# Way up of both MLPs as pairs of column groups in seven block products

## The chip, the cores and the metric

The program runs on one NeuronCore of a Trainium2 chip, in one launch. The metric is the device time of that core in microseconds (us). In the rows PE is TensorE (matmuls; PEld its weight loads), DVE is VectorE, ACT is ScalarE, POOL is GpSimd, and SP is the engine that issues most DMAs.

## The reference, cut to what matters

Two layers work on 640 tokens (128 of a context, 512 of a latent grid) of width 1024, with different weights per layer. A layer is three parallel mixers, an output projection, and a gated MLP:

```python
xn2 = rmsnorm(x, norm2) * (1 + scale2) + shift2
u = dwconv3(xn2 @ w_up, ffn_conv_w)          # w_up: 1024 x 5632, conv of width 3 over positions
a, bval = u[..., :D_FF], u[..., D_FF:]       # D_FF = 2816
x = x + gate2 * ((jax.nn.silu(a) * bval) @ w_down)
```

`shift2`, `scale2` and `gate2` come from a conditioning vector times `w_ada` (6144 columns per layer), one set for the context and one for the grid. All is float32.

## The kernel before

Activations lie with channels on the 128 partitions and the 640 tokens along the free axis: `x` is eight tiles [128, 640]. Each float32 operand of a product is split into two float32r parts, high and low, and a product is three matmuls: high weights by high input (L150), high by low (L151), low by high (L152). The tokens go in two halves of 320, the columns of one matmul. A piece of weights [128, 512] (four blocks of 128 rows of the contraction) comes by DMA into `wraw` (4 buffers); `split` (L114 to L116) makes `whi` on ScalarE and then `wlo = wraw - whi` on VectorE (6 buffers each).

The MLP (from L1017) goes in four parts of `FFPARTS`. In each part it computes the way up of 5 or 6 pairs of column groups, a gate group and its value group of 128 columns each, and then the way down from those tiles. Group by group, `up_half` puts eight blocks times three matmuls per half of the tokens into a PSUM tile `f`. `ffn_conv` (L806 to L810) takes it from PSUM: ScalarE scales it by the middle tap into `u`, and VectorE adds the other two taps, for the 128 and the 512 tokens apart. `ffn_act` makes silu on ScalarE, the product (L816) on VectorE, and the split `fh`, `fl` for the way down.

At the start of an MLP the output projection has just ended for the second half of the tokens. The first half of the normalised input is made during that projection (`norm_steps`, tiles `Xh`, `Xl`). For the second half, a few matmuls by ones add up the squares (L231), a chain of small VectorE instructions takes their inverse root (L213 to L219), a matmul spreads it (L243), and `norm_tile` writes the tiles one after the other. Meanwhile TensorE takes the first half of three groups (`lead`).

In the mixers of layer 0 and in its MLP, VectorE also computes modulations (`ada_rows`, L312): a step is one DMA of weights into `wraw` and two multiply-and-sum instructions, 84 steps in layer 0's mixers and 76 in its MLP.

The program is written with tile pools, and a scheduler sets each engine's order when it is built. At run time every engine takes its instructions in that order and waits on semaphores. So an instruction whose input is late holds up all that stands behind it on its engine.

## Time and profile before

| | |
|---|---|
| median of 3 runs | 2590.2 us (2588.8 to 2591.19) |
| profiled execution | span 2587.0 us from first to last instruction; the page gives no other time of it |
| TensorE, ScalarE, VectorE, GpSimd busy | 2536.4, 1067.8, 1698.1, 131.5 us |
| MLP of layer 0, of layer 1, first matmul of the way up to the end of the way down | about 456 us and 458 us |

What lies outside the span, median of the runs less span, is 3.2 us. A matmul's duration includes its way through the array and overlaps with that of its neighbours: durations of matmuls can't be added up, their starts tell the pace. On VectorE too, the next instruction can start before the last has ended; "slot" below means the time from one start to the next.

### The profile page before, as it was taken

What the parts mean: (1) busy time and instruction counts of PE and PEld (TensorE: products, weight loads), DVE (VectorE), ACT (ScalarE), POOL (GpSimd) and SP (SyncE); (2) the same over time, 40 slices, a digit from 0 to 9 for tenths busy, and PEclk for the clock granted to TensorE, in tenths of its full rate; (3) what the DMA queues carried; (4) which work ended last, traced back from release to release, by engine and by line L of the source; (5) the groups of instructions that cost most, each with busy time, mean ns of one, the idle gap of its engine ahead of it and who ended that gap; (6) DMA issues with size and microseconds to landing.
All of it is one profiled execution on the core that took longest, in us unless ns stands there. A gap on an engine that the chain in (4) does not pass through costs nothing. (4 is left out here: it accounts for less than half of the span.)

```text
span 2587.0 us, 44571 instructions
## 1 busy us (share of the span) xinstructions
PE 2536.4 (98%) x17422; PEld 2481.9 (96%) x17422; DVE 1698.1 (66%) x3627; ACT 1067.8 (41%) x2108; POOL 131.5 (5%) x113
## 2 busy tenths in 40 slices
PE   7999999999999999999999999999999999999998
PEld 3999999999999999999999999999999999999998
DVE  5677787787765878787667675555554466554555
ACT  3476733433324423232355666434333343233332
POOL 1000000000111000000010000000011110000001
PEclk8999999999999999999999999999999999999999
DMA  6211243333343334443331112212222312322221
GB/s 232 73 46 45 67 134 111 103 115 108 118 155 102 106 116 136 133 124 124 96 112 53 38 50 70 66 57 63 64 64 85 116 55 60 93 66 83 66 86 62
DMA packets 138597, 236.17 MB, mean 91 GB/s; under 512 B 16465, under 2 KB 34321, under 8 KB 138257
## 3 DMA queue, kind: packets, MB, share of 16 engines
q1 hardware_dynamic: 133778, 222.83, 27.9%
q10 hardware_dynamic: 4608, 10.49, 1.2%
q8 instruction: 137, 2.24, 0.3%
q14 instruction: 74, 0.61, 0.1%
HBM read 226.67 MB, written 6.59 MB: 90 GB/s over the span
## 5 line engine op out<-in xcount | busy, mean ns | idle before, releaser
L116 DVE TENSOR_TENSOR wlo<-wraw,whi 128x512 fp32r<-128x512 f32 (+1 forms) x620 | 407.9, 662 | 379.7 <-ACT whi L115 372.4
L115 ACT CAST whi<-wraw 128x512 fp32r<-128x512 f32 (+1 forms) x620 | 364.4, 592 | 659.8 <-PE f L151 345.7
L150 PE MATMUL lin<-Xh,whi 128*128 128x320 f32 x1920 | 605.3, 315 | 3.9 <-DVE th L573 2.6
L151 PE MATMUL lin<-Xl,whi 128*128 128x320 f32 x1920 | 595.7, 310 | 0.0
L152 PE MATMUL lin<-Xh,wlo 128*128 128x320 f32 x1920 | 595.6, 310 | 0.0
L150 PE MATMUL f<-Xh,whi 128*128 128x320 f32 x1408 | 435.4, 309 | 0.0
L151 PE MATMUL f<-Xl,whi 128*128 128x320 f32 x1408 | 435.2, 309 | 0.0
L152 PE MATMUL f<-Xh,wlo 128*128 128x320 f32 x1408 | 435.1, 309 | 0.0
L150 PEld LDWEIGHTS lin<-Xh,whi 128*128 128x128 f32 x1920 | 361.5, 188 | 5.4 <-DVE th L573 3.7
L151 PEld LDWEIGHTS lin<-Xl,whi 128*128 128x128 f32 x1920 | 361.8, 188 | 0.0
L152 PEld LDWEIGHTS lin<-Xh,wlo 128*128 128x128 f32 x1920 | 361.2, 188 | 0.0
L151 PEld LDWEIGHTS f<-Xl,whi 128*128 128x128 f32 x1408 | 264.3, 188 | 0.1
L150 PEld LDWEIGHTS f<-Xh,whi 128*128 128x128 f32 x1408 | 264.3, 188 | 0.0
L152 PEld LDWEIGHTS f<-Xh,wlo 128*128 128x128 f32 x1408 | 264.3, 188 | 0.0
L151 PE MATMUL f<-fl,whi 128*128 128x320 f32 x604 | 186.2, 309 | 0.0
L152 PE MATMUL f<-fh,wlo 128*128 128x320 f32 x604 | 185.2, 309 | 0.0
L150 PE MATMUL f<-fh,whi 128*128 128x320 f32 x604 | 182.2, 310 | 0.0
L312 DVE SCALAR_TENSOR_TENSOR ad<-wraw,rows 128x512 f32<-128x512 f32 x168 | 119.8, 713 | 47.5 <-DMA wraw<-in_w_rows 45.4
L312 DVE SCALAR_TENSOR_TENSOR pr<-wraw,rows 128x512 f32<-128x512 f32 x152 | 104.5, 688 | 26.0 <-DMA wraw<-in_w_rows 24.2
L150 PE MATMUL lin<-yh,whi 128*128 128x320 f32 x384 | 120.5, 314 | 0.7 <-ACT th L567 0.7
L152 PE MATMUL lin<-yh,wlo 128*128 128x320 f32 x384 | 118.8, 309 | 0.0
L151 PE MATMUL lin<-yl,whi 128*128 128x320 f32 x384 | 118.6, 309 | 0.0
(275 smaller groups left out, 4440.0 us busy)
## 6 DMA issues: line engine op xcount, KB each, us to landing
wraw<-in_w_main SPq DMA_DIRECT2D x456, 256.0 KB, 2.6
wraw<-in_w_rows SPq DMA_DIRECT2D x160, 256.0 KB, 2.7
wraw<-in_w_down SPq DMA_DIRECT2D x64, 256.0 KB, 2.7
wraw<-in_w_o SPq DMA_DIRECT2D x48, 256.0 KB, 2.6
ada<-in_w_ada SPq DMA_DIRECT2D x24, 256.0 KB, 6.0
x<-in_xT ACTq DMA_DIRECT2D x16, 320.0 KB, 3.3
wraw<-in_w_down SPq DMA_DIRECT2D x32, 128.0 KB, 2.1
wraw<-in_w_q SPq DMA_DIRECT2D x16, 192.0 KB, 2.3
```

Of the source, the lines that this page charges most:

```text
L115: S.copy(hi, x)
L116: V.tensor_tensor(lo, x, hi.bitcast(F32), ALU.subtract)
L150: PE.matmul(o, wh, xh[:, half(j)], start=(k == 0), stop=False)
L151: PE.matmul(o, wh, xl[:, half(j)], start=False, stop=False)
L152: PE.matmul(o, wl, xh[:, half(j)], start=False, stop=(k == n - 1))
L312: V.scalar_tensor_tensor(spare(), raw, 1.0, rows[:, s], ALU.mult, ALU.mult, accum_out=part[:, j, m - m0, s:s + 1])
```

## The change

A pair's two groups are computed together. The pair's weights are four blocks `wa`, `wb` (gate group, first and second half of the contraction) and `wc`, `wd` (value group); the normalised input is four blocks `B11`, `B21` (first half of the tokens; first and second half of the contraction) and `B12`, `B22`. Instead of eight block products, seven are made (a block product is 4 blocks of contraction times 3 matmuls): `wa`·`B11`, `wb`·`B21`, (`wa+wc`)·`T3`, (`wa+wc+wd`)·`t2`, `wd`·`T4`, (`wc+wd`)·`t1`, (`wa+wb+wc+wd`)·`B22`, where `T3`, `t2`, `T4`, `t1` are sums and differences of the blocks of input. Two PSUM banks, `Y` and `Z`, collect several of them, and what they hold in between is read out on the way.

- The sums of weights are four VectorE additions per pair, and seven pieces of weights are split instead of four. Pairs 0 to 2 of a layer (`LEAD`) load `wb` twice.
- Results are put together in SBUF (`o0`, `o1`, `z`): five ScalarE copies from PSUM and three VectorE instructions per pair. `ffn_conv` then reads SBUF and not PSUM.
- `Forms` makes the blocks of input: `first` during the output projection, `second` (with all sums and differences and ten splits of 640 columns) for the second half of the tokens, before any of the way up in program order.
- Of the modulations, 64 steps go from layer 0's MLP to layer 1's mixers; 12 stay.
- In the last part of a way down, five column tiles' weights are loaded and split again for the second half of the tokens instead of being kept.

```diff
@@
+DMA_ADDS = False
+LEAD = 3
...
-        BUFS = {"mla": {"sc": 2, "pt": 2}, "hgrn": {"sc": 2, "m": 1, "ad": 1}, "ffn": {"f": 3}}
+        BUFS = {"mla": {"sc": 2, "pt": 2}, "hgrn": {"sc": 2, "m": 1, "ad": 1}, "ffn": {"Y": 2, "Z": 2, "X": 2}}
...
+    KH = KD // 2
+    def form_tile(pool, dt, tag, name, bufs):
+        return pool.tile([P, 2, HALF], dt, tag=tag, name=name, bufs=bufs)
+    def norm_raw(l, which, sq, j, f, e, i, bc):
+        for s0, s1, s in SEGS[j]:
+            b0, b1 = s0 - j * HALF, s1 - j * HALF
+            V.scalar_tensor_tensor(f[:, e, b0:b1], x[i][:, s0:s1], amul[l][:, which, i, s:s + 1],
+                                   bc[:, b0:b1], ALU.mult, ALU.mult)
+            S.activation(f[:, e, b0:b1], f[:, e, b0:b1], AF.Identity, bias=modT[l][:, 24 * which + i, s:s + 1])
+    class Forms:
+        def __init__(self, l, which, sq, xf):
+            self.l, self.which, self.sq, self.xf = l, which, sq, xf
+            self.f = {n: [None, None] for n in ("B11", "B21", "B22", "t1", "t2", "T3", "T4")}
+            self.raw = {}
+        def put(self, name, q, f):
+            if name in ("t2", "T3", "T4"):
+                hi = form_tile(self.xf, R32, "Fh", "Fh", 6)
+                lo = form_tile(self.xf, R32, "Fl", "Fl", 6)
+            else:
+                hi = form_tile(mp, R32, "Xh", "Xh", 8)
+                lo = form_tile(mp, R32, "Xl", "Xl", 8)
+            split(f, hi, lo)
+            self.f[name][q] = (hi, lo)
+        def operand(self, name):
+            return [(self.f[name][r // 2][0][:, r % 2], self.f[name][r // 2][1][:, r % 2]) for r in range(KH)]
+        def first(self):
+            bc = self.sq.rstd(0)
+            for q in range(2):
+                for n, name in enumerate(("B11", "B21")):
+                    f = form_tile(mp, F32, "Xl", "xn", 8)
+                    for e in range(2):
+                        norm_raw(self.l, self.which, self.sq, 0, f, e, KH * n + 2 * q + e, bc)
+                        yield
+                    self.put(name, q, f)
+                    self.raw[name, q] = f
+        def second(self, pool):
+            bc = self.sq.rstd(1)
+            raw = self.raw
+            for q in range(2):
+                for n, name in enumerate(("B12", "B22")):
+                    f = raw[name, q] = form_tile(pool, F32, "fh", "xn", 7)
+                    for e in range(2):
+                        norm_raw(self.l, self.which, self.sq, 1, f, e, KH * n + 2 * q + e, bc)
+                f = raw["T3", q] = form_tile(pool, F32, "fl", "xs", 7)
+                V.tensor_tensor(f, raw["B22", q], raw["B12", q], ALU.subtract)
+                self.put("T3", q, f)
+            for q in range(2):
+                f = raw["t2", q] = form_tile(pool, F32, "fl", "xs", 7)
+                V.scalar_tensor_tensor(f, raw["T3", q], -1.0, raw["B11", q], ALU.mult, ALU.subtract)
+                self.put("t2", q, f)
+            for q in range(2):
+                f = raw["t2", q]
+                V.scalar_tensor_tensor(f, f, -1.0, raw["B21", q], ALU.mult, ALU.subtract)
+                self.put("T4", q, f)
+            for q in range(2):
+                f = raw["B12", q]
+                V.tensor_tensor(f, raw["B11", q], f, ALU.subtract)
+                self.put("t1", q, f)
+            for q in range(2):
+                self.put("B22", q, raw["B22", q])
+            raw.clear()
+    def part_product(o, W, X, start, stop):
+        wh, wl = W
+        for k, (xh, xl) in enumerate(X):
+            c = slice(k * P, (k + 1) * P)
+            PE.matmul(o, wh[:, c], xh, start=start and k == 0, stop=False, skip_group_check=True)
+            PE.matmul(o, wh[:, c], xl, start=False, stop=False, skip_group_check=True)
+            PE.matmul(o, wl[:, c], xh, start=False, stop=stop and k == KH - 1, skip_group_check=True)
+    def pair_steps(l, g, F, pool, lead, banks, evict):
+        wa, wb, wc, wd = (a["w_main"][l, gg, j] for gg in (g, g + 1) for j in range(2))
+        def load(src, own=False):
+            t = (pool.tile([P, 512], F32, tag="T", name="T", bufs=LEAD) if own else
+                 wp.tile([P, 512], F32, tag="wraw", name="wraw", bufs=RAWB))
+            nc.sync.dma_start(t, src)
+            return t
+        def form(t):
+            hi = wp.tile([P, 512], R32, tag="whi", name="whi", bufs=WB)
+            lo = wp.tile([P, 512], R32, tag="wlo", name="wlo", bufs=WB)
+            split(t, hi, lo)
+            return hi, lo
+        def add(t, src, tile=None):
+            if DMA_ADDS:
+                G.dma_start(t, src, accum_op=ALU.add)
+            else:
+                V.tensor_tensor(t, t, tile, ALU.add)
+        h0, h1 = half(0), half(1)
+        o0 = pool.tile([P, T], F32, tag="o", name="o", bufs=4)
+        t = load(wa, True)
+        Y = banks[0]()
+        part_product(Y, form(t), F.operand("B11"), True, False)
+        S.copy(o0[:, h0], Y)
+        rb = None
+        def second():
+            nonlocal rb
+            rb = load(wb)
+            X = banks[1]()
+            part_product(X, form(rb), F.operand("B21"), True, True)
+            V.tensor_tensor(o0[:, h0], X, o0[:, h0], ALU.add)
+        if lead:
+            second()
+        yield
+        o1 = pool.tile([P, T], F32, tag="o", name="o", bufs=4)
+        rc = load(wc)
+        add(t, wc, rc)
+        Z = banks[2]()
+        part_product(Z, form(t), F.operand("T3"), True, False)
+        z = pool.tile([P, HALF], F32, tag="z", name="z", bufs=2)
+        S.copy(z, Z)
+        if not lead:
+            second()
+        rd = load(wd)
+        add(t, wd, rd)
+        part_product(Y, form(t), F.operand("t2"), False, False)
+        S.copy(o1[:, h0], Y)
+        part_product(Z, form(rd), F.operand("T4"), False, True)
+        V.scalar_tensor_tensor(o1[:, h0], Z, -1.0, o1[:, h0], ALU.mult, ALU.subtract)
+        add(rc, wd, rd)
+        part_product(Y, form(rc), F.operand("t1"), False, False)
+        S.copy(o1[:, h1], Y)
+        V.scalar_tensor_tensor(o1[:, h1], o1[:, h1], -1.0, z, ALU.mult, ALU.subtract)
+        if lead and not DMA_ADDS:
+            rb = load(wb)
+        add(t, wb, rb)
+        W = form(t)
+        evict(1, o1)
+        yield
+        part_product(Y, W, F.operand("B22"), False, True)
+        S.copy(o0[:, h1], Y)
+        evict(0, o0)
+        yield
...
+                    else:
+                        steps = ada_rows(1, 16, 48, zp, lambda: ps.one("ad"))
...
-                    X = new_X()
-                    first = norm_steps(l, 1, sq, 0, X)
+                    first = F.first()
             run(first)
             hq.__exit__(None, None, None)
             ps.phase("ffn")
-            run(norm_steps(l, 1, sq, 1, X))
-        npool = pool_of("np0")
-        sq = Squares(npool.__enter__())
         with pool_of("fp") as fp:
+            F.second(fp)
+            sq = Squares(sq.pool)
             steps = iter(())
             if l == 0:
-                steps = ada_rows(1, ADA1, 48, fp, lambda: fp.tile([P, 512], F32, tag="pr", name="pr"))
+                steps = ada_rows(1, ADA1, 16, fp, lambda: fp.tile([P, T], F32, tag="u", name="pr", bufs=3)[:, 0:512])
             fconv = fp.tile([P, 3, 2 * NFF], F32, name="fconv")
             nc.sync.dma_start(fconv, a["fconv"][:, l])
-            Ys, us = [], []
-            def done(g, o):
-                us.append(ffn_conv(g, o, fp, fconv))
-                if len(us) == 2:
-                    Ys.append(ffn_act(us[0], us[1], fp))
-                    us.clear()
+            Ys = []
+            def bank(tag):
+                return lambda: (ps.bank() if tag == "lin" else ps.one(tag))[:, 0:HALF]
+            def up_pair(j):
+                us = {}
+                def evict(s, o):
+                    us[s] = ffn_conv(s * NFF + j, o, fp, fconv)
+                    if s == 0:
+                        Ys.append(ffn_act(us[0], us[1], fp))
+                return pair_steps(l, G_UP + 2 * j, F, fp, j < LEAD,
+                                  [bank(t) for t in (("Y", "X", "Z") if j != 2 else ("lin", "lin", "Z"))], evict)
+            ups = [up_pair(j) for j in range(NFF)]
+            for j in range(LEAD):
+                next(ups[j])
             for pi, (k0, k1) in enumerate(FFPARTS):
                 last = pi == len(FFPARTS) - 1
-                # the first tile of the next part goes ahead of this part's way down
-                groups = [(s * NFF + j, 2 * j + s) for j in range(k0 + (pi > 0), k1 + (not last)) for s in range(2)]
-                lead = 3 if pi == 0 else 0
-                held = []
-                for g, wg in groups[:lead]:
-                    W = weights(w_main(l, G_UP + wg))
-                    o = ps.two("f")
-                    up_half(W, X, o, 0)
-                    held.append((g, W, o))
-                for g, W, o in held:
-                    up_half(W, X, o, 1)
-                    done(g, o)
-                for i, (g, wg) in enumerate(groups[lead:]):
-                    W = weights(w_main(l, G_UP + wg))
-                    o = ps.two("f")
-                    for j in range(2):
-                        up_half(W, X, o, j)
-                    done(g, o)
-                    run(steps, UPR[i % len(UPR)])
+                for j in range(k0 + (pi > 0), k1 + (not last)):
+                    next(ups[j])
+                    if LEAD <= j + 1 < NFF:
+                        next(ups[j + 1])
+                    run(ups[j])
+                    run(steps, 1)
                 if l == 0 and last:
                     run(steps)
                     ada_scale(1, 0)
-                    ada_scale(1, 1)
                 W, Y = {}, Ys[k0:k1]
                 for j in range(2):
                     for m in both_ways(j) if last else range(KD):
-                        if j == 0:
+                        if j == 0 or 0 <= m <= KEEP - 1:
                             srcs = [a["w_down"][l, m][:, k * P:min(k + 4, k1) * P] for k in range(k0, k1, 4)]
-                            W[m] = weights(srcs, (fp, KEEP) if last and 0 < m <= KEEP else None)
-                        f = ps.two("f")
-                        run(steps, DNR[m % len(DNR)])
+                            W[m] = weights(srcs)
+                        run(steps, 1)
                         for jj in ((j,) if last else (0, 1)):
-                            o = f[:, 512 * jj:512 * jj + HALF]
+                            o = ps.any()
```

The scheduler orders the engines anew. TensorE at the end of layer 0's output projection (`Hh`, `Hl` times kept weights), the sums of squares and the first matmuls of the way up, before:

```order
L151 MATMUL lin<-Hl,khi 128x320
L152 MATMUL lin<-Hh,klo 128x320
L231 MATMUL lin<-ones,acc 128x2
L150 MATMUL f<-Xh,whi 128x320
L151 MATMUL f<-Xl,whi 128x320
L152 MATMUL f<-Xh,wlo 128x320
L150 MATMUL f<-Xh,whi 128x320
L151 MATMUL f<-Xl,whi 128x320
L152 MATMUL f<-Xh,wlo 128x320
```

and now:

```order
L151 MATMUL lin<-Hh,keep 128x320
L239 MATMUL lin<-ones,acc 128x2 x6
L473 MATMUL Y<-Xh,whi 128x320
L474 MATMUL Y<-Xl,whi 128x320
L473 MATMUL X<-Xh,whi 128x320
L474 MATMUL X<-Xl,whi 128x320
L475 MATMUL Y<-Xh,wlo 128x320
L473 MATMUL Y<-Xh,whi 128x320
L474 MATMUL Y<-Xl,whi 128x320
L251 MATMUL lin<-dg,ones 128x128 x3
L475 MATMUL Y<-Xh,wlo 128x320
L473 MATMUL Y<-Xh,whi 128x320
```

All six sums of squares now stand directly behind the projection, and after four matmuls of the way up stands one that reads `wlo`; before, twelve matmuls of the way up stood ahead of the other five sums.

VectorE at the same place, from the end of the chain for the inverse root on, before (`pr` are modulations, `nt` and `Xl` the normalised tiles):

```order
L218 SCALAR_TENSOR_TENSOR rs_t<-rs_t,rs_m 128x3
L219 SCALAR_TENSOR_TENSOR rs_r<-rs_t,rs_r 128x3
L312 SCALAR_TENSOR_TENSOR pr,part_9862<-wraw,rows 128x512
L237 TENSOR_TENSOR dg<-ident,rs_r 128x384
L312 SCALAR_TENSOR_TENSOR pr,part_9862<-wraw,rows 128x512
L362 SCALAR_TENSOR_TENSOR nt<-x,amul_79,lin 128x320 x3
L368 SCALAR_TENSOR_TENSOR Xl<-nt,mod_77,Xh 128x320
L362 SCALAR_TENSOR_TENSOR nt<-x,amul_79,lin 128x320
L368 SCALAR_TENSOR_TENSOR Xl<-nt,mod_77,Xh 128x320
L362 SCALAR_TENSOR_TENSOR nt<-x,amul_79,lin 128x320 x3
L368 SCALAR_TENSOR_TENSOR Xl<-nt,mod_77,Xh 128x320
L362 SCALAR_TENSOR_TENSOR nt<-x,amul_79,lin 128x320
```

and now, from the last two tiles of the second half (`xn`) on; the first three `wlo` of the way up and six `xn` stand ahead of this piece:

```order
L405 SCALAR_TENSOR_TENSOR xn<-x,amul_79,lin 128x320 x2
L463 TENSOR_TENSOR xn<-xn 128x640
L117 TENSOR_TENSOR Fl<-xs,Fh 128x640
L451 TENSOR_TENSOR xs<-xn 128x640
L455 SCALAR_TENSOR_TENSOR xs<-xs,xn 128x640 x2
L117 TENSOR_TENSOR Fl<-xs,Fh 128x640 x3
L459 SCALAR_TENSOR_TENSOR xs<-xs,xn 128x640 x2
L117 TENSOR_TENSOR Xl<-xn,Xh 128x640
L117 TENSOR_TENSOR Fl<-xs,Fh 128x640 x2
L463 TENSOR_TENSOR xn<-xn 128x640
L513 TENSOR_TENSOR o<-X,o 128x320
L117 TENSOR_TENSOR wlo<-wraw,whi 128x512
```

Before, the low halves of the weights for the lead stood ahead of the chain; now the fourth of them stands behind most of the sums, differences and splits of 640 columns (`xs`, `Fl`, `Xl`), and the fifth and sixth behind three more of them.

VectorE for one pair in the middle of layer 1's MLP, before, the whole of it:

```order
L116 TENSOR_TENSOR wlo<-wraw,whi 128x512 x2
L808 SCALAR_TENSOR_TENSOR u<-f,fconv,u 128x127
L810 SCALAR_TENSOR_TENSOR u<-f,fconv,u 128x127
L808 SCALAR_TENSOR_TENSOR u<-f,fconv,u 128x511
L810 SCALAR_TENSOR_TENSOR u<-f,fconv,u 128x511
L116 TENSOR_TENSOR wlo<-wraw,whi 128x512 x2
L808 SCALAR_TENSOR_TENSOR u<-f,fconv,u 128x127
L810 SCALAR_TENSOR_TENSOR u<-f,fconv,u 128x127
L808 SCALAR_TENSOR_TENSOR u<-f,fconv,u 128x511
L810 SCALAR_TENSOR_TENSOR u<-f,fconv,u 128x511
L816 TENSOR_TENSOR u<-u 128x640
L116 TENSOR_TENSOR fl<-u,fh 128x640
```

and now, half of it (`o<-X`, `o<-Z`, `o<-o,z` put results together, `T` and `wraw` as target are the sums of weights):

```order
L972 SCALAR_TENSOR_TENSOR u<-o,fconv,u 128x127
L972 SCALAR_TENSOR_TENSOR u<-o,fconv,u 128x511
L513 TENSOR_TENSOR o<-X,o 128x320
L117 TENSOR_TENSOR wlo<-T,whi 128x512
L978 TENSOR_TENSOR u<-u 128x640
L497 TENSOR_TENSOR T<-T,wraw 128x512
L497 TENSOR_TENSOR wraw<-wraw 128x512
L117 TENSOR_TENSOR fl<-u,fh 128x640
L531 SCALAR_TENSOR_TENSOR o<-Z,o 128x320
L117 TENSOR_TENSOR wlo<-T,whi 128x512
L117 TENSOR_TENSOR wlo<-wraw,whi 128x512
L535 SCALAR_TENSOR_TENSOR o<-o,z 128x320
```

A pair has 24 VectorE instructions now and had 14, and the low half for a later product (`wlo`) stands behind instructions that wait for earlier products.

## Rows read from the trace of the kernel before

**Rows 1.** The page: span; busy us (share); a group (count | busy, mean ns).

```profile
span 2587.0 us, 44571 instructions
...
PE 2536.4 (98%) x17422; PEld 2481.9 (96%) x17422; DVE 1698.1 (66%) x3627; ACT 1067.8 (41%) x2108; POOL 131.5 (5%) x113
...
L150 PE MATMUL f<-Xh,whi 128*128 128x320 f32 x1408 | 435.4, 309 | 0.0
```

**Rows 2.** Stretches: us, busy us (count) by engine, PEclk, DMA share, GB/s.

```profile
315.00:843.60 528.60, 523.10 (x3682) 519.60 (x3681) 379.53 (x837) 199.05 (x388) 44.57 (x30) 1.00 0.37 117
1581.20:2101.80 520.60, 519.97 (x3679) 518.95 (x3678) 271.56 (x495) 198.64 (x388) 44.57 (x30) 1.00 0.24 73
843.60:1300.00 456.40, 456.09 (x3112) 455.10 (x3111) 349.64 (x800) 155.25 (x261) 7.65 (x8) 1.00 0.38 119
2101.80:2560.00 458.20, 457.79 (x3124) 456.76 (x3123) 259.23 (x498) 155.50 (x258) 7.66 (x8) 1.00 0.24 71
```

**Rows 3.** Timeline, VectorE, layer 1: start, duration, engine, line, tiles [idle <-releaser].

```profile
2245.75 0.69 DVE L116 TENSOR_TENSOR wlo<-wraw,whi 128x512 fp32r<-128x512 f32 x1 [1.07 <-ACT whi L115]
2246.45 0.35 DVE L808 SCALAR_TENSOR_TENSOR u<-f,fconv,u 128x127 f32<-128x127 f32 x1
2246.84 0.35 DVE L810 SCALAR_TENSOR_TENSOR u<-f,fconv,u 128x127 f32<-128x127 f32 x1
2247.10 0.74 DVE L808 SCALAR_TENSOR_TENSOR u<-f,fconv,u 128x511 f32<-128x511 f32 x1
2247.88 0.75 DVE L810 SCALAR_TENSOR_TENSOR u<-f,fconv,u 128x511 f32<-128x511 f32 x1
...
2257.32 0.83 DVE L116 TENSOR_TENSOR fl<-u,fh 128x640 fp32r<-128x640 f32 x1 [0.79 <-ACT fh L115]
2258.07 0.69 DVE L116 TENSOR_TENSOR wlo<-wraw,whi 128x512 fp32r<-128x512 f32 x1
...
2260.53 0.35 DVE L808 SCALAR_TENSOR_TENSOR u<-f,fconv,u 128x127 f32<-128x127 f32 x1
```

**Rows 4.** Timeline, VectorE in a way down of layer 1.

```profile
2203.18 0.55 DVE L396 SCALAR_TENSOR_TENSOR x<-f,mod,x 128x320 f32<-128x320 f32 x1 [2.60 <-PE f L152]
2203.64 0.69 DVE L116 TENSOR_TENSOR wlo<-wraw,whi 128x512 fp32r<-128x512 f32 x1
2204.24 0.67 DVE L396 SCALAR_TENSOR_TENSOR x<-f,mod,x 128x128 f32<-128x128 f32 x2
```

**Rows 5.** Timeline, TensorE at the start of layer 0's MLP.

```profile
843.63 0.39 PE L150 MATMUL f<-Xh,whi 128*128 128x320 f32 x1
...
845.47 1.19 PE L231 MATMUL lin<-ones,acc 128*128 128x2 f32 x10
```

**Rows 6.** Timeline, VectorE at the same place.

```profile
843.69 0.55 DVE L396 SCALAR_TENSOR_TENSOR x<-lin,mod,x 128x320 f32<-128x320 f32 x1 [1.88 <-PE lin L152]
...
846.70 0.16 DVE L234 TENSOR_SCALAR rs_m<-lin 128x3 f32<-128x3 f32 x1 [1.37 <-PE lin L231]
...
848.87 0.16 DVE L219 SCALAR_TENSOR_TENSOR rs_r<-rs_t,rs_r 128x3 f32<-128x3 f32 x1
```

**Rows 7.** Groups by form, VectorE, layer 1's MLP (columns as rows 1).

```profile
L116 DVE TENSOR_TENSOR wlo<-wraw,whi 128x128 fp32r<-128x128 f32 x11 | 3.2, 287 | 3.0 <-ACT whi L115 3.0
...
L344 DVE TENSOR_TENSOR acc<-acc,sq 128x320 f32<-128x320 f32 x2 | 1.0, 492 | 1.2 <-ACT sq L343 1.2
```

**Rows 8.** Groups by form, VectorE, layer 0's MLP: modulations.

```profile
L312 DVE SCALAR_TENSOR_TENSOR pr<-wraw,rows 128x512 f32<-128x512 f32 x152 | 104.5, 688 | 26.0 <-DMA wraw<-in_w_rows 24.2
...
L312 DVE DVE_READ_ACCUMULATOR pr<-wraw,rows 128x1 f32 x152 | 12.6, 83 | 0.0
```

**Rows 9.** Stretches at the program's end (columns as rows 2).

```profile
2574.00:2578.00 4.00, 1.47 (x10) 1.39 (x9) 2.07 (x13) 0.00 (x0) 0.00 (x0) 0.55 0.00 0
2578.00:2582.00 4.00, 1.62 (x6) 1.35 (x6) 2.20 (x5) 0.00 (x0) 0.00 (x0) 0.50 0.09 30
```

More of the change, by code (lines that the diff above doesn't have):

```diff
@@ L198, in one @@
         def one(tag="m"):
-            if ps.name == "ffn":
+            if ps.name == "ffn" and tag == "m":
                 return ps.bank()
@@ L208, in wide, with any @@
             return ps.two("sc")
+        turn = 0
+        @staticmethod
+        def any():
+            ps.turn += 1
+            tag = ("lin", "X", "Z", "Y")[ps.turn % 4]
+            return (ps.bank() if tag == "lin" else ps.one(tag))[:, 0:HALF]
     def rsqrt_small(out, m, n):
@@ L991, in hybrid_flow_kernel, with kept @@
                         V.scalar_tensor_tensor(hl, h_acc[m], 0.5, hh.bitcast(F32), ALU.mult, ALU.subtract)
-                    if l == 0:
-                        run(steps)
-                        ada_scale(0, 1)
-        with pool_of("np2") as pool, pool_of("wo") as wo:
-            sq = Squares(pool)
+                    run(steps)
+                    ada_scale(l, 1)
+        xf_ = pool_of("xf")
+        xf = xf_.__enter__()
+        F = Forms(l, 1, sq, xf)
+        def kept(m):
+            if not 0 < m <= KEEP:
+                return None
+            pool, tags, n = (xf, "F", 6) if m <= 3 else (wo, "k", 4)
+            return lambda: [pool.tile([P, T], R32, tag=tags + t, name="keep", bufs=n) for t in "hl"]
+        with pool_of("wo") as wo:
             W = {}
```

15 lines of the change are left out of this document (6 added, 9 removed).

## The prediction

> **What bounds the kernel now.** I read the page's first lines, then stretches by engine, then the starts in the timelines, because durations of matmuls mislead here. TensorE is busy for 98% of the span, VectorE for 66% [rows 1]. In both MLPs TensorE has no idle time worth the name (456.09 of 456.40 us; 457.79 of 458.20), though VectorE is busy for 350 us in layer 0's and 259 us in layer 1's [rows 2]. So TensorE sets the time, and what other engines do costs nothing as long as it is in time.
>
> The pace of TensorE is not the mean of 309 ns [rows 1]: one pair of column groups takes from 2246.45 to 2260.53, 14.08 us [rows 3], for 2 groups x 8 blocks x 3 x 2 halves = 96 matmuls, so 0.1467 us each. In that time VectorE does 14 instructions and idles before several of them, as the releasers in the rows show.
>
> **What the change takes away.** A block product is 12 matmuls, and each of 22 pairs in 2 layers makes seven instead of eight: 44 x 12 x 0.1467 = **77.4 us** off TensorE. A pair then needs 84 x 0.1467 = 12.32 us of it. The 64 modulation steps that leave layer 0's MLP give nothing back there, since TensorE didn't wait for them.
>
> **What VectorE must do per pair.** I take slots, from one start to the next. A [128, 512] instruction from SBUF: 0.60 (2203.64 to 2204.24), 320 columns from PSUM: 0.46 (2203.18 to 2203.64) [rows 4]. Of 640 columns: 0.75 (2257.32 to 2258.07) [rows 3]. 128 columns from SBUF take 0.287 against 0.35 from PSUM, 320 from SBUF 0.49 [rows 3, 7]; less the overlap of 0.09 that the other slots show, that is 0.20 and 0.40. The new additions [128, 512] don't occur in the trace; nearest is the low half with the same two sources and shape, and I take its 0.60 (bounds: 0.60, and 0.69 with no overlap).
>
> Then a pair now costs: 7 low halves and 4 sums, 11 x 0.60 = 6.6; two results from PSUM 0.92, one from SBUF 0.40; the taps 4 x 0.60 + 4 x 0.20 = 3.2; product and split of 640 columns 1.5. Together **12.6 us** of bare slots, against TensorE's 12.32. To this come waits: after the product, the split waits for ScalarE's high half (0.79 idle in [rows 3], of which one instruction of 0.60 now covers most, so 0.25); the taps wait for ScalarE's scaling, likewise 0.25; instructions that need the one just before start about 0.12 later than bare slots (0.78 from one 511-wide tap to the next, 0.745 long [rows 3]), about three times. So 0.85 more, 13.5 in all: VectorE becomes the slower of the two by about 1.1 us a pair, and what it gains during the way down decides.
>
> A page of the Trainium skill speaks against the overlap: "VectorE: DVE Perf Modes", section Terms, says that the pipeline is flushed after every operation before the next can issue. The starts above disagree, 0.08 or 0.09 us before the end of the instruction ahead where its result isn't needed [rows 3, 4]. By the rule, 24 durations would be added end to end; what that gives is the second rival's case.
>
> **The start of each MLP.** Here TensorE was covered by half products of three groups; now three things fall on it. (a) All six sums of squares stand right behind the projection, and the fourth matmul after them wants nothing late but the fifth a `wlo`, which stands behind the chain for the inverse root. From the projection's end (843.63) [rows 5] to the chain's end (848.87 + 0.16) [rows 6] and one low half (0.62) are 6.0 us, in which TensorE has sums and four matmuls, 1.3 us: idle 4.7, two layers **9.4**. That no earlier sum would help is seen in the rows: last addition to `x` at 843.69, sums at 845.47, chain from 846.70.
>
> (b) From there to the first product of pair 6 VectorE's queue holds, in layer 1, 160 instructions: 66 low halves and weight sums (39.6), 28 of 640 columns, of which 18 make the blocks of input (21.0), 20 from PSUM of 320 (9.2), 5 from SBUF (2.0), the taps, 20 x 0.60 + 20 x 0.20 (16.0), and the diagonal for the inverse root 0.5: 88.3 us. TensorE has 495 matmuls up to there, 72.6. It falls behind by 15.7, nearly all of it at once: between the third and the fourth low half of the lead lie 24 instructions (8 of 320 from PSUM, 15 of 640, and one result), 16.0 us with the half itself, and TensorE has some 35 matmuls (5.1). Layer 0 adds 12 multiply-and-sum instructions of modulations, 0.69 + 0.08 long [rows 8], slot 0.75: 24.7. Both layers **40.4**. (c) The waits of 0.85 for six pairs and about 1.0 between the engines in the sums of input: 6.1 per layer, **12.2** (0 if all are hidden).
>
> **The later parts.** During a way down VectorE has time (the idle 2.60 in [rows 4] before each `x`), and in the order the first pair's seven low halves, about 7.3 us with the sums, stand there. Not all of that is a lead, since the low half for the next pair's first product stands right behind `o<-Z`, which waits for a product of this pair; I count 2 us of it as free. That covers the 1.1 us of the second and the third pair. So in parts of 6, 6 and 4 pairs the first three run at TensorE's pace, and each further one is late by most of the 1.1, say 0.8 us: 2.4 + 2.4 + 0.8, **11.2** for both layers. Below it can be 0; above, if the lead is lost in waits, 32 pairs at VectorE's pace (second rival).
>
> **Layer 1's mixers** take on 64 steps. Layer 0's mixers with 84 steps take 528.6 us, layer 1's without any 520.6, with the same work else and TensorE idle for 5.5 and 0.6 us [rows 2]. That is 0.095 a step: **6.1** (bounds: 0, and 8.0; nothing can be gained, as TensorE doesn't idle there now).
>
> **At no cost**: the loads (three or four of 256 KB per pair, with the DMA engines at 0.24 of their time in layer 1's MLP [rows 2]); ScalarE's three more casts and five copies per pair (it is busy for 155 of 456 us); the five tiles split again in the last way down (VectorE idles there). If ScalarE's strict order should hold a copy of `Y` up, the next product into that bank waits; that is part of the 0.85.
>
> **Sum.** -77.4 + 9.4 + 40.4 + 12.2 + 11.2 + 6.1 = +1.9 us on a span of 2587.0, 2588.9; with the 3.2 us by which the runs' median lies above the span, **2592 us**. The saving is real and the start of the two MLPs, with the wait for VectorE's queue, eats it.
>
> **Rivals.**
> 1. *Faster: VectorE keeps up.* The waits (c) and those of the later parts are hidden by the low halves made ahead (six buffers, 6 x 1.76 us of products). For it: six buffers are more than any single wait above. Against: in the order each pair's low halves stand behind instructions that wait for the pair before. The time: 2592 - 12.2 - 11.2 = 2569; with the mixers free too, 2563.
> 2. *Slower: the two engines in lock-step.* VectorE's queue waits for TensorE's products and TensorE for its low halves, and the lead from the way down is gone after the first pair. It decides from a pair of about 14 us on, when the free 2 us are used up at once. By whole durations (the page's rule) it is 11 x 0.69 + 2 x 0.55 + 0.49 + 4 x 0.69 + 4 x 0.29 + 2 x 0.83 = 14.8. With 14.1, as long as before, the later 32 pairs save nothing: 32 x 1.76 = 56 instead of 11 is lost, 2637; with 14.8 another 22.
> 3. *Slower: the clock.* After TensorE has idled in the program's end its granted clock is 0.55 and then 0.50, the lower of the two levels, 1.2 GHz [rows 9]; it may fall in the idle stretch of about 11 us of (b). If it stays low for the three lead pairs, 210 matmuls take 0.1467 more each, 31 us, of which VectorE's queue hides about half: 15 per layer, 2622. The Trainium skill, "TensorE: Matmul & The Clock Gate", Part 1, says that activity brings the clock back; by that the loss would be a few matmuls, hidden behind VectorE's queue. No row here shows a return after such a gap.
>
> **Chances.** The forecast, 2580 to 2607 in its own range, 0.48; the first rival 0.27; the second 0.15; the third 0.07; the rest, 0.03, beyond all of these. 0.2% (5 us) is what a measurement of this kernel can tell from none. Of the forecast's 0.48, 0.05 lies below 2585, 0.23 within 5 us and 0.20 above: faster 0.32, same 0.23, slower 0.45. The range that leaves out 2 in 10 goes from 2565 to 2628.
>
> **What would show it.** In the profile after: 528 matmuls fewer; 14.08 us per pair turned into 12.3 to 13.5 in the middle of layer 1's MLP; idle time of TensorE of about 5 us before and some 11 us after the third low half of each lead, released by `wlo`; VectorE busy for over 90% in the first part; MLPs of about 459 us in layer 0 and 452 in layer 1; layer 1's mixers some 6 us longer. I am wrong if the starts of the two MLPs cost less than 20 us in all, or if pairs in later parts still take 14 us.

## The result, and the profile after

The median of four runs is 2625.0 us (2624.6 to 2630.3); the kernel before, on the same chip, 2589.7 (2588.8 to 2591.2). The ratio is 1.0142, 95% interval 1.0127 to 1.0156: **1.4% slower**. The prediction's 2592 missed this by 33 us; its range, 2565 to 2628, just held it.

The page after, in the form of [rows 1] (span; busy us by engine, share, count):

```profile
span 2628.5 us, 44321 instructions
PE 2505.1 (95%) x16894; PEld 2424.5 (92%) x16894; DVE 1948.2 (74%) x4109; ACT 1239.4 (47%) x2492; POOL 117.7 (4%) x97
```

The 528 matmuls are gone (17422 to 16894), and TensorE's span grew all the same. Where, the stretches show. I cut both kernels at the same matmuls: the last one of the output projection, the first and the last one of the way down. First before (columns as in [rows 2]):

```profile
0.00:843.60 843.60, 814.44 (x5542) 775.88 (x5543) 599.32 (x1329) 380.56 (x794) 56.83 (x48) 0.99 0.34 108
843.60:930.40 86.80, 86.77 (x596) 86.42 (x595) 71.97 (x164) 36.09 (x59) 4.17 (x4) 1.00 0.33 104
930.40:1314.60 384.20, 383.17 (x2612) 382.26 (x2612) 291.48 (x674) 128.95 (x226) 8.96 (x13) 1.00 0.40 126
1314.60:2101.80 787.20, 778.72 (x5459) 765.56 (x5459) 461.89 (x926) 363.90 (x766) 50.33 (x36) 1.00 0.22 67
2101.80:2188.60 86.80, 86.67 (x596) 86.39 (x595) 55.02 (x104) 36.48 (x59) 4.16 (x4) 1.00 0.21 59
2188.60:2571.90 383.30, 383.02 (x2613) 382.27 (x2612) 211.12 (x408) 121.38 (x204) 7.01 (x8) 1.00 0.25 75
```

and the same stretches after:

```profile
0.00:852.70 852.70, 820.19 (x5542) 779.03 (x5542) 593.51 (x1319) 377.73 (x788) 52.26 (x44) 0.99 0.34 104
852.70:971.10 118.40, 90.77 (x536) 85.02 (x535) 104.51 (x202) 64.69 (x117) 0.00 (x0) 0.88 0.27 84
971.10:1342.70 371.60, 361.41 (x2408) 353.71 (x2406) 308.55 (x624) 186.34 (x361) 10.25 (x13) 1.00 0.30 89
1342.70:2139.20 796.50, 782.44 (x5460) 767.97 (x5458) 540.43 (x1180) 364.98 (x766) 47.25 (x33) 0.99 0.30 89
2139.20:2245.00 105.80, 84.94 (x514) 80.67 (x513) 95.12 (x175) 62.52 (x113) 0.00 (x0) 0.89 0.24 70
2245.00:2613.80 368.80, 362.19 (x2430) 355.42 (x2430) 298.75 (x588) 182.71 (x349) 7.96 (x8) 1.00 0.28 83
```

A stretch's **loss** below is its length less its matmuls times 0.1467 us, the pace of the prediction (good to about half a microsecond, since some small matmuls are counted along). Before, an MLP loses nothing (384.2 - 2612 x 0.1467 = 1.0, the others 0). After:

| stretch | length before, after | loss after | predicted |
|---|---|---|---|
| to the end of layer 0's projection | 843.6, 852.7 | | 0 |
| layer 0, way up ahead of the first way down | 86.8, 118.4 | 39.8 | 35.5 (a, b, c) |
| layer 0, the rest of the MLP | 384.2, 371.6 | 18.3 | 5.6 |
| layer 1's mixers | 787.2, 796.5 (+9.3) | | +6.1 |
| layer 1, way up ahead of the first way down | 86.8, 105.8 | 30.4 | 26.5 (a, b, c) |
| layer 1, the rest of the MLP | 383.3, 368.8 | 12.3 | 5.6 |

The first stretch's 9.1 us belong to this execution, the slowest of the four: in seven profiles of the experiments with the same instructions there it is between 841.4 and 845.8.

**The start of an MLP** went nearly as drawn. TensorE there, layer 0, answers to [rows 5]:

```profile
852.48 0.31 PE L151 MATMUL lin<-Hh,keep 128*128 128x320 f32 x1
...
854.53 1.28 PE L239 MATMUL lin<-ones,acc 128*128 128x2 f32 x10 [1.61 <-DVE acc L352]
856.21 0.63 PE L473 MATMUL Y<-Xh,whi 128*128 128x320 f32 x1 [0.41 <-ACT whi L116]
...
858.84 0.64 PE L475 MATMUL Y<-Xh,wlo 128*128 128x320 f32 x1 [1.19 <-DVE wlo L117]
...
878.23 0.64 PE L475 MATMUL X<-Xh,wlo 128*128 128x320 f32 x1 [10.94 <-DVE wlo L117]
```

The wait behind the third low half is 10.9 us ("about 11"), released by `wlo`; the three waits ahead of it add up to 3.2 us, where (a) had 4.7. VectorE, just before, is at the forms of the input without a pause, then comes the low half:

```profile
870.48 2.29 DVE L117 TENSOR_TENSOR Fl<-xs,Fh 128x640 fp32r<-128x640 f32 x3
...
877.09 0.48 DVE L513 TENSOR_TENSOR o<-X,o 128x320 f32<-128x320 f32 x1
877.50 0.68 DVE L117 TENSOR_TENSOR wlo<-wraw,whi 128x512 fp32r<-128x512 f32 x1
```

The third rival's clock shows as well (stretches, columns as in [rows 2]):

```profile
870.00:878.20 8.20, 0.00 (x0) 0.00 (x0) 8.20 (x13) 3.69 (x6) 0.00 (x0) 0.50 0.00 0
878.20:884.00 5.80, 5.77 (x23) 5.60 (x24) 5.73 (x10) 1.90 (x4) 0.00 (x0) 0.57 0.28 90
884.00:890.00 6.00, 6.00 (x43) 6.00 (x42) 3.86 (x7) 3.22 (x7) 0.00 (x0) 1.00 0.30 88
```

In the wait the granted clock is 0.50, the lower level (1.2 GHz); when TensorE works again it makes 23 matmuls in 5.8 us, and 43 in the next 6.0, at the upper one. So the clock is back long before the three pairs of the lead are done; it falls once more behind a later wait (0.83 from 910 to 920 us).

**A later part.** The starts of `o<-Z` on VectorE tell the pairs of the second part of layer 1 apart:

```profile
2290.71 0.49 DVE L531 SCALAR_TENSOR_TENSOR o<-Z,o 128x320 f32<-128x320 f32 x1 [0.45 <-PE Z L475]
...
2328.25 0.49 DVE L531 SCALAR_TENSOR_TENSOR o<-Z,o 128x320 f32<-128x320 f32 x1
2343.13 0.49 DVE L531 SCALAR_TENSOR_TENSOR o<-Z,o 128x320 f32<-128x320 f32 x1 [0.83 <-PE Z L475]
2356.42 0.49 DVE L531 SCALAR_TENSOR_TENSOR o<-Z,o 128x320 f32<-128x320 f32 x1
```

Five pairs in 65.7 us, 13.1 each and 14.9 for the longest, against 14.08 in [rows 3] and 12.32 of TensorE's work. The stretch with the late ones:

```profile
2311.00:2361.00 50.00, 48.00 (x315) 45.86 (x314) 48.08 (x89) 32.55 (x60) 0.00 (x0) 1.00 0.28 84
```

VectorE is busy for 48.1 of 50 us, and TensorE loses 50 - 315 x 0.1467 = 3.8. Ahead of the first way down VectorE is busy for 88% (104.51 of 118.40 us) and 90% (95.12 of 105.80) of the stretch; the prediction had said over 90%.

**The end of layer 0** held something the prediction did not look at. TensorE before:

```profile
1314.42 0.31 PE L152 MATMUL f<-fh,klo 128*128 128x320 f32 x1
1314.56 0.31 PE L150 MATMUL lin<-Xh,whi 128*128 128x320 f32 x1
...
1316.03 0.39 PE L150 MATMUL sc<-Xh,whi 128*128 128x320 f32 x1
...
1324.54 0.71 PE L243 MATMUL pt<-dg,ones 128*128 128x128 f32 x4 [1.73 <-DVE dg L237]
```

and after:

```profile
1342.59 0.31 PE L151 MATMUL Y<-fh,wlo 128*128 128x320 f32 x1
1344.92 1.68 PE L239 MATMUL pt<-ones,acc 128*128 128x2 f32 x12 [2.03 <-DVE acc L352]
1349.62 1.65 PE L251 MATMUL pt<-dg,ones 128*128 128x128 f32 x6 [3.02 <-DVE dg L245]
1350.92 0.61 PE L149 MATMUL sc<-Xh,whi 128*128 128x320 f32 x1
```

Before, products of layer 1's first half (`lin<-Xh`, `sc<-Xh`) ran while VectorE made the inverse root for the second; now they stand behind it, and TensorE waits 5 us. VectorE is not later with the first half's tiles (`nt`) than it was: the last row of them starts 1.65 us after the way down's last product before, and 1.48 us after it now (before, then after):

```profile
1316.07 0.66 DVE L362 SCALAR_TENSOR_TENSOR nt<-x,amul,lin 128x128 f32<-128x128 f32 x2
```

```profile
1344.07 0.40 DVE L370 SCALAR_TENSOR_TENSOR nt<-x,amul,lin 128x192 f32<-128x192 f32 x1
```

So it is the order of TensorE's instructions that changed there.

### The profile page after: what moved, and what is told of

It is laid out like the page before. It is cut to its first block, busy times and chain, and to the rows that moved or that the text cites. A ratio compares the mean times of both kernels' runs of the same rounds, so it can differ in the third digit from the quotient of the medians.

```text
span 2628.5 us, 44321 instructions
## 1 busy us (share of the span) xinstructions
PE 2505.1 (95%) x16894; PEld 2424.5 (92%) x16894; DVE 1948.2 (74%) x4109; ACT 1239.4 (47%) x2492; POOL 117.7 (4%) x97
## 4 chain that ended last, share of the span: by engine, by line
PE 69%; DVE 20%; ACT 4%; DMA 4%; issue 3%; POOL 1%; DVEq 0%; ACTq 0%; SPq 0%; POOLq 0%
PE lin L149 13%; PE lin L150 13%; PE lin L151 13%; DVE wlo L117 5%; PE sc L901 2%; DVE u L970 2%; PE sc L636 2%; DVE u L972 2%; DMA wraw<-in_w_rows 2%; PE pt L927 2%; PE Y L475 2%; PE pt L918 2%; DVE ad L320 1%; ACT whi L116 1%; PE Y L473 1%
## 5 line engine op out<-in xcount | busy, mean ns | idle before, releaser
L473 PE MATMUL Y<-Xh,whi 128*128 128x320 f32 x504 | 158.3, 314 | 4.3 <-ACT whi L116 2.4
L475 PE MATMUL Y<-Xh,wlo 128*128 128x320 f32 x504 | 157.8, 313 | 1.8 <-DVE wlo L117 1.8
L116 ACT CAST whi<-T 128x512 fp32r<-128x512 f32 x176 | 106.7, 618 | 107.8 <-DVE T L497 46.1
L474 PE MATMUL Y<-Xl,whi 128*128 128x320 f32 x504 | 156.8, 311 | 0.0
L117 DVE TENSOR_TENSOR wlo<-T,whi 128x512 fp32r<-128x512 f32 x176 | 118.9, 685 | 24.7 <-ACT whi L116 24.1
L475 PE MATMUL Z<-Fh,wlo 128*128 128x320 f32 x352 | 111.3, 316 | 8.0 <-DVE wlo L117 8.0
L473 PE MATMUL Z<-Fh,whi 128*128 128x320 f32 x352 | 110.6, 314 | 0.0
L474 PE MATMUL Z<-Fl,whi 128*128 128x320 f32 x352 | 109.3, 311 | 0.0
L473 PEld LDWEIGHTS Y<-Xh,whi 128*128 128x128 f32 x504 | 95.7, 190 | 7.3 <-ACT o L534 3.3
L475 PEld LDWEIGHTS Y<-Xh,wlo 128*128 128x128 f32 x504 | 95.6, 190 | 3.4 <-DVE wlo L117 2.9
```

What stands on the lines that cost most here:

```text
L116: S.copy(hi, x)
L117: V.tensor_tensor(lo, x, hi.bitcast(F32), ALU.subtract)
L473: PE.matmul(o, wh[:, c], xh, start=start and k == 0, stop=False, skip_group_check=True)
L474: PE.matmul(o, wh[:, c], xl, start=False, stop=False, skip_group_check=True)
L475: PE.matmul(o, wl[:, c], xh, start=False, stop=stop and k == KH - 1, skip_group_check=True)
```

## The experiments

Two theories. **A, amount**: VectorE has more to do per pair than TensorE, its backlog sets the time, and what it is relieved of comes back. **B, order and latency**: the waits come from where instructions stand, the latency of single sums, or the clock. Ratios are to the kernel before on the same chip.

**1. Sums of weights left out.**

```diff
-                V.tensor_tensor(t, t, tile, ALU.add)
+                pass
```

> The four additions of weights per pair are left out (the pieces are split unsummed, so the products are of other numbers; loads, splits, products and all waits for the loads stay). Theory A, the amount of VectorE's work sets the way up: 176 additions of about 0.60 us leave, and VectorE's queue up to pair 6 of layer 1 shrinks from 88.3 to 73.9 us against 72.6 of TensorE, a later pair from about 13.3 to 10.9 us against 12.3. Then some 14 us per layer at the start and nearly all of the 4 us per later part come back: 2575 to 2585 us, against 2625 with the additions. Theory B, order and latency set it (six low halves of the lead behind the forms of the input, the chain of the inverse root, the clock): the idle time of 11 us after the third low half and the loss around the later parts stay, and only the latency of one addition per wait goes, 5 to 10 us in all: 2615 to 2620 us.

2572.1 us, ratio 0.9941 (0.9926 to 0.9956). A: 176 additions less, and 53 us come back. Layer 1's MLP:

```profile
2099.90:2197.50 97.60, 85.64 (x536) 83.16 (x535) 84.19 (x160) 64.61 (x119) 0.00 (x0) 0.90 0.29 85
2197.50:2553.60 356.10, 354.79 (x2409) 352.24 (x2408) 255.14 (x515) 182.34 (x342) 7.98 (x8) 1.00 0.28 83
```

The loss ahead of the first way down falls from 30.4 to 97.6 - 536 x 0.1467 = 19.0, later from 12.3 to 2.7. That what stays at the start comes with the forms and the inverse root is the prediction's reading; this run doesn't show it.

**2. The sums on GpSimd.** `G.tensor_tensor` in place of `V.tensor_tensor` in the same line.

> The same four additions per pair on GpSimd instead of VectorE, result unchanged. An addition of 128x512 took no row there; GpSimd's 128x320 take 0.98 us and its 128x640 1.65 to 1.90 us, so about 1.4 us is my estimate, 0.8 more than on VectorE, 5.6 us of GpSimd per pair of 12.3. Theory A (amount of VectorE's work): the same relief as without additions, less some waits: 2578 to 2595 us. Theory B (latency of the chain load, sum, high half, low half): every sum comes 0.8 us later and the waits of TensorE grow: 2630 to 2650 us.

2689.6 us, ratio 1.0396 (1.0381 to 1.0412), outside both. Groups in layer 1's MLP, GpSimd first, then two of VectorE (count | busy, mean ns of one):

```profile
L497 POOL TENSOR_TENSOR T<-T,wraw 128x512 f32<-128x512 f32 x66 | 105.8, 1604 | 307.4 <-DVE wlo L117 193.6 <-issue 110.7 <-DMA wraw<-in_w_main 3.1
```

```profile
L117 DVE TENSOR_TENSOR wlo<-wraw,whi 128x512 fp32r<-128x512 f32 x100 | 84.7, 849 | 17.8 <-ACT whi L116 17.8
...
L535 DVE SCALAR_TENSOR_TENSOR o<-o,z 128x320 f32<-128x320 f32 x22 | 27.1, 1233 | 0.0
```

In the changed kernel the same two:

```profile
L117 DVE TENSOR_TENSOR wlo<-wraw,whi 128x512 fp32r<-128x512 f32 x100 | 68.6, 696 | 17.1 <-ACT whi L116 16.9
...
L535 DVE SCALAR_TENSOR_TENSOR o<-o,z 128x320 f32<-128x320 f32 x22 | 10.7, 484 | 0.3
```

A sum takes 1.60 us instead of 0.69, and VectorE's instructions become longer while GpSimd adds: 0.85 for 0.70, 1.23 for 0.48. TensorE now waits for ScalarE (62.5 us in 28 waits for a copy `o` before a product into `Y`):

```profile
PE Y L473 <- ACT o L534: 62.5, 28, 3.4
```

ScalarE's copy stands behind a high half that waits for GpSimd's sum (in layer 1's MLP ScalarE's high halves wait for `T` 37 times, 66.6 us in all). The Trainium skill, "SBUF — State Buffer", section "Who interferes with whom", says that a VectorE instruction with two SBUF inputs contends with a GpSimd instruction that reads SBUF; both groups above have two, and the trace agrees.

**3. The lead first.**

```diff
             bc = self.sq.rstd(1)
+            yield
...
-            F.second(fp)
-            sq = Squares(sq.pool)
+            rest = F.second(fp)
+            next(rest)
...
             for j in range(LEAD):
                 next(ups[j])
+            run(rest)
+            sq = Squares(sq.pool)
```

> In program order the six pieces of weights of the lead now stand ahead of the second half of the tokens' normalised tiles and all forms, so all six products of the lead can run before VectorE's 24 instructions of forms. Work is the same. Theory A (amount): TensorE does 36 matmuls (5.3 us) earlier and then waits that much longer for the first sum of weights; pair 6 starts when VectorE's queue is done, as before: 2620 to 2627 us. Theory B (order): the 5.3 us per layer are won and with them part of the slow clock behind the idle stretch (5.0 us per layer): 2605 to 2615 us.

2622.0 us, ratio 1.0135 (1.012 to 1.015): A. All six products of the lead ran first, and the first product of a sum of weights then started 10.1 us after the matmul before it; layer 1's first stretch is 106.9 us long and was 105.8.

**4. Matmuls in the gap.**

```diff
...
+            for _ in range(fill if k == 0 else 0):
+                PE.matmul(o, zero, xh, start=False, stop=False, skip_group_check=True)
...
```

> Sixty matmuls with weights of zero go into the lead's fourth product, right where TensorE idles 11 us for the fourth low half, so that it doesn't idle there (60 x 0.1467 = 8.8 us); results are unchanged. After the idle stretch the granted clock is 0.50 for about 13.7 us of the record and TensorE's matmuls there take twice their pace, 5.0 us more per layer. Theory A (VectorE's queue decides, so the slow stretch is hidden behind it): no gain, 2622 to 2627 us. Theory B (the clock is a cost of its own): the 5.0 us per layer come back, 2612 to 2616 us.

2619.9 us, ratio 1.0132 (1.0115 to 1.0149). The granted clock stayed up where the wait had been (what is left of it is in this row, with 29 matmuls in 6 us):

```profile
870.00:876.00 6.00, 4.51 (x29) 4.25 (x30) 5.93 (x10) 2.04 (x4) 0.00 (x0) 1.00 0.31 87
```

and layer 1's first stretch still took 106.7 us (105.8), layer 0's 117.7 (118.4). The low clock in this gap lies within VectorE's backlog. The time falls between the two forecasts; the ratio's fall by 0.001 is within both intervals, which leave no room for the 10 us of theory B. The clock was not up everywhere: over layer 1's first stretch it was 0.94 on average, and 0.89 in the changed kernel.

**5. Weights of the last way down kept**, as before the change.

```diff
-                        if j == 0 or 0 <= m <= KEEP - 1:
+                        if j == 0:
...
-                            W[m] = weights(srcs)
+                            W[m] = weights(srcs, kept_down() if last and 0 < m <= KEEP else None)
```

(`kept_down` hands out the buffers of `T3`, `t2` and `T4`.)

> The five column tiles of the last way down keep their split weights for the second half of the tokens again, in the buffers of the forms that are dead by then; ten low halves per layer leave VectorE (5 x (0.60 + 0.20) = 4.0 us per layer), the rest is unchanged. Theory A: these splits, which the prediction costed at nothing, delay the normalised first half at the end of layer 0, so that TensorE stands still for the chain of the inverse root with no products of the next layer ahead of it (4.7 us at the boundary), and cost about 2 us in each last way down: 2614 to 2618 us. Theory B: the cover is missing because the next layer's input tiles now share buffers with the forms, and the splits cost nothing: 2622 to 2627 us.

2608.3 us, ratio 1.0088 (1.0073 to 1.0103): A, and more than I gave it. The end of layer 0:

```profile
1331.02 0.31 PE L151 MATMUL lin<-fh,keep 128*128 128x320 f32 x1
1331.17 0.31 PE L149 MATMUL sc<-Xh,whi 128*128 128x320 f32 x1
```

The cover is back; the stretch to layer 1's projection is 790.4 us (796.5), the rest of the MLPs 368.6 and 367.2 (371.6, 368.8).

**6. No modulations in an MLP.** `ADA1 = 16` for 10, and the call for steps 10 to 15 left out there.

> The 12 modulation steps left in layer 0's MLP go to layer 0's mixers too, so that both MLPs do the same work. Theory A, amount of VectorE's work: layer 0's way up and down lost 58.8 us of TensorE's pace, layer 1's 43.3; the difference of 15.5 comes back, less 12 x 0.095 = 1.1 us in the mixers: 2609 to 2613 us. By the prediction's own size (24 instructions of 0.75 less the cover, 9.0 us) 2616 to 2618 us. Theory B, they fall into waits: 2624 to 2627 us.

2606.2 us, ratio 1.0081 (1.0066 to 1.0096): A. Layer 0's MLP:

```profile
845.70:951.00 105.30, 84.42 (x514) 80.23 (x513) 95.08 (x175) 62.56 (x113) 0.00 (x0) 0.89 0.23 70
951.00:1320.40 369.40, 362.46 (x2430) 355.44 (x2428) 302.18 (x600) 188.08 (x365) 10.33 (x13) 1.00 0.28 85
```

With 474.7 us for 490.0 it is like layer 1's. Twelve steps cost 15.3 us: 9.9 of the loss ahead of the first way down (39.8, now 105.3 - 514 x 0.1467 = 29.9) and 5.4 of the rest (18.3, now 369.4 - 2430 x 0.1467 = 12.9). The prediction had 9.0 for those ahead of it, and nothing for those behind.

**7. Five parts.** `FFPARTS = ((0, 5), (5, 9), (9, 13), (13, 17), (17, 22))`.

> Five parts of 5, 4, 4, 4 and 5 pairs instead of four of 5, 6, 6 and 5; same products, one more round of additions to x per layer on VectorE (about 8 x 1.1 us), eight fewer small splits per part of four. Theory A: VectorE falls behind pair by pair and the way down lets it catch up by a fixed lead; with four pairs the lead lasts, and the losses of 4 us around pairs 4 to 6 of a part (12.6 us in layer 1, 18.7 in layer 0, with the last way down) fall by half or more: 2607 to 2615 us. Theory B: the loss belongs to the change between way up and way down, whatever the number of pairs; one more of them per layer costs 4 us each: 2630 to 2635 us.

2607.6 us, ratio 1.0082 (1.0067 to 1.0097): A. The rest of layer 1's MLP:

```profile
2227.40:2589.20 361.80, 359.18 (x2429) 355.31 (x2429) 307.53 (x604) 181.66 (x341) 7.95 (x8) 1.00 0.28 84
```

Its loss is 361.8 - 2429 x 0.1467 = 5.5 (12.3). The lead from a way down lasts four pairs; the fifth and sixth were late.

**8. Before, with the 64 modulation steps moved.**

```diff
+                    else:
+                        steps = ada_rows(1, 16, 48, zp, lambda: ps.one("ad"))
...
-                steps = ada_rows(1, ADA1, 48, fp, lambda: fp.tile([P, 512], F32, tag="pr", name="pr"))
+                steps = ada_rows(1, ADA1, 16, fp, lambda: fp.tile([P, 512], F32, tag="pr", name="pr"))
...
```

> The kernel before with the 64 modulation steps moved from layer 0's MLP to layer 1's mixers and nothing else. Prediction: 64 x 0.095 = 6.1 us slower, 2594 us. By the profile of the changed kernel, where layer 1's mixers took some 4 us more: 2591 to 2593 us. If the steps find idle time in VectorE in both places: 2587 to 2589 us.

2589.0 us, ratio 1.0011 (1.0001 to 1.0021): 2.9 us (0.3 to 5.4). The 6.1 were too many.

**9. The sums by DMA.** `DMA_ADDS = True`.

> The changed kernel's own switch: the four sums of weights per pair are made by DMAs that add a piece in DRAM to the one in SBUF, issued by GpSimd; VectorE and GpSimd do no addition. Theory A (amount of VectorE's work): the same relief as leaving them out, 2572 to 2590 us. Theory B (what made the additions on GpSimd slow was that each sum came late, 1.61 us instead of 0.69, with ScalarE's copies queued behind the wait): a DMA lands 2.8 us after its issue, later still, so the time is as bad as there or worse, 2680 us and up. If it comes out near A, the harm on GpSimd was VectorE's slower instructions (0.85 us per low half instead of 0.70), not the latency.

2816.2 us, ratio 1.0884 (1.0867 to 1.0901): B, for sums that come this late. The DMAs that add into `T` (count, size, median us from issue to landing), and what GpSimd's queue waited for:

```profile
T<-in_w_main POOLq DMA_DIRECT2D x132, 256.0 KB, 4.7
```

```profile
POOL T L495 <- DVE wlo L117: 561.8, 106, 19.7
```

A plain load into `T` lands after 2.6 us in this run. Each sum waits in GpSimd's one queue until VectorE has split the one before. `wlo` from `T` takes 0.69 us here, as on the changed kernel, so in the second experiment it was GpSimd's adding that made VectorE slower.

**10. The fifth, sixth and seventh together.**

> Five parts, kept weights in the last way down and no modulations in the MLPs, together. Each alone took the ratio to the kernel before from 1.0142 to 1.0082, 1.0088 and 1.0081. If they act at different places, as the theory of VectorE's amount has it (pairs 4 to 6 of a part; the end of the way down; layer 0's first part), the gains add up: ratio 0.997, about 2579 us. If they are three ways to the same gain, 1.005 or more, 2600 us.

2586.1 us, ratio 0.9995 (0.9986 to 1.0004): as fast as before, where 0.997 was expected if the gains add up in full. Together they give 0.0147 of the 0.0175 that they gave alone. Layer 1's MLP:

```profile
2102.40:2209.30 106.90, 85.57 (x514) 81.37 (x514) 95.15 (x176) 62.55 (x113) 0.00 (x0) 0.89 0.23 69
2209.30:2568.80 359.50, 358.81 (x2431) 355.34 (x2430) 302.83 (x594) 177.23 (x331) 7.56 (x8) 1.00 0.27 80
```

The rest loses 2.9 us; 31.5 are left ahead of the first way down, and 3.5 and 32.0 in layer 0.

**11. These, with the sums by DMA.**

> The three of the run before and the sums by DMA. Theory A: of the first part's loss of 30 us per layer some 10 are left out by the relief too (as without additions, where it was 19 to 24), the rest of the later losses is gone already: 2555 to 2565 us, the fastest so far. Theory B, latency of the sums: no better than without the three, above 2650 us.

2775.3 us, ratio 1.0726 (1.0711 to 1.074): B, as in the ninth.

**12. Eight products for pairs 0 to 3.**

```diff
+    def group_steps(l, g, F, pool, tag, evict):
+        W = weights(w_main(l, g))
+        o = pool.tile([P, T], F32, tag="o", name="o", bufs=4)
+        for j in range(2):
+            b = ps.one(tag)[:, 0:HALF]
+            group_half(W, b, F, j)
+            S.copy(o[:, half(j)], b)
...
+                    if j < N8:
+                        for q in gs[2 * j:2 * j + 2]:
+                            run(q)
+                        run(forms, 1)
```

(For room, `fh` and `fl` have 6 buffers instead of 7 and `T` 2 instead of 3.)

> The three of the combination, and pairs 0 to 3 of each layer by eight block products (no sums of weights, four low halves instead of seven, results only copied by ScalarE; their operands B12 and B22 come right after the norm, and the sums of the input, T3, t2, T4 and t1, are made behind pairs 0 to 2 in program order). Theory A, amount of VectorE's work: in the combination each layer loses some 31 us before its first way down. Four pairs of eight products cost TensorE 4 x 1.76 = 7.0 us per layer and take 4 x 5.5 = 22 us from VectorE there, so that its queue up to pair 6 is shorter than TensorE's: the 31 us become 7.0 and 2 to 4 of waits, 2586 - 2 x 21 = 2544 us (2538 to 2556). Theory B, the loss belongs to the chain of the inverse root and to making the forms, wherever they stand: it stays and 7.0 us per layer come on top, 2595 to 2602 us.

2560.8 us, ratio 0.9904 (0.9887 to 0.992): **1% faster than before**, A. Layer 1's MLP:

```profile
2090.30:2174.20 83.90, 83.61 (x572) 82.87 (x571) 72.62 (x135) 53.10 (x96) 0.00 (x0) 1.00 0.20 60
2174.20:2542.80 368.60, 363.72 (x2422) 355.30 (x2420) 299.94 (x589) 175.17 (x327) 8.19 (x8) 1.00 0.26 78
```

The first stretch loses nothing, and the clock stays up. The edit takes work from VectorE there and also puts the sums of the input behind the first pairs; the two were not tried apart. The rest loses 13.3, where the tenth lost 2.9; with that it would have been near the 2544 expected. There TensorE's listed waits are for ScalarE, its copies (2.7 us in 6) and its high halves (1.5 in 4); they don't account for all of the 13.3, and whether the fewer buffers cause it was not tried.

## Why the prediction came out as it did

- **The matmuls** (-77.4): right. 528 are gone, and where TensorE doesn't wait the loss by the old pace is nothing (83.9 us for 572 matmuls in the twelfth experiment).
- **The start of each MLP** (9.4 + 40.4 + 12.2 = 62.0): right in place, cause and nearly in size. Both layers lost 39.8 + 30.4 = 70.2, with the wait of 10.9 us where it was expected. That it is VectorE's amount and not the place of the six low halves is shown by the third experiment (order changed, time not) and the first (amount changed, 30.4 became 19.0 in layer 1); in the twelfth, which changes amount and order, the loss is gone. The surplus is about 4 us in each layer (4.3 and 3.9), so it doesn't come from the modulations, which only layer 0 has: their 9.9 here are near the 9.0 counted. Where it comes from stays open.
- **The later parts** (11.2): the step that failed most. They lost 18.3 + 12.3 less the 1.0 of before, 29.6, which is 18.4 more. Two terms stood at nothing: the modulations behind the first way up's end (5.4, sixth experiment) and the splits of the next point (4.6 of these stretches, fifth experiment). The other 8.4 are late pairs. "I count 2 us of it as free. That covers the 1.1 us of the second and the third pair", with 0.8 for each further one, was too kind: the last pairs of a part of six lost 3.8 us instead of 2.4, and with five parts (seventh experiment) the two layers lose 12.1 + 5.5, 13.0 less.
- **"At no cost": five tiles split again in the last way down, since VectorE idles there.** Wrong, shown by the fifth experiment: the stretches that it changed are 10.7 us shorter. With the splits in VectorE's queue beside the next layer's normalised tiles, the products that had covered the inverse root before stand behind it; without them they stand ahead again. Why the scheduler orders them so was not looked at; the tiles themselves came no later. It is term (a) at a third place, and the order of TensorE's instructions there would have shown it.
- **Layer 1's mixers** (6.1): too large. 3.2 us are left in that stretch once the weights are kept (790.4 against 787.2), and the move alone cost 2.9 (0.3 to 5.4). The 0.095 a step came from the difference of two layers' mixers, put down to the modulations as a whole; why fewer cost so much less was not tried.
- **Rivals.** The first, that VectorE keeps up, failed. The second, lock-step from a pair of 14 us on, was not reached: 13.1. The third rival's clock fell at the place it named; its price was wrong, since the clock was back soon, and the fourth experiment took the low clock out of the gap and the stretch stayed as long. That its 2622 lies near the measured time is chance. The Trainium skill's rule ("TensorE: Matmul & The Clock Gate", Part 1) that activity brings the clock back agrees with the 23 and then 43 matmuls above.

Together: first stretches +8.2, the rest of the MLPs +18.4, mixers with the boundary +3.2, 30 of the 33 us by which 2592 fell short. The MLPs took 490.0 and 474.6 us, where 459 and 452 were expected. The forecast's own range, 2580 to 2607, missed the time by 18 us. The wide range held it because it made room for the second and third rival, and neither happened; that much was luck.

## What to carry to other kernels

A change that takes work from the engine that bounds and gives other work to a second engine is priced stage by stage from the second one's queue: 66% busy over the span was 88 and 90% ahead of each first way down and 96% in a later stretch that got the work. What made it pay here was to even out the second engine's load (smaller parts, no side work in the busy stage, the old form where the queue is already full), and not to move its place or its clock. When anything is moved or split again near a place where TensorE waits for a short chain, look in its order whether the products that covered the chain still stand ahead of it.
